# The conditioning rows of an RWKV gate, moved from the early pairs of heads to the later ones

## The chip, the cores and the metric

The kernel runs on one core of a Trainium2 chip. Its metric is the device time of one execution in microseconds (us), the median over runs. Engines are named as in the profile: PE is TensorE (matmuls; PEld is its weight load), DVE is VectorE, ACT is ScalarE, POOL is GpSimd, SP is SyncE, which here issues nearly all DMAs. Q behind a name (SPq, PEq) is the engine's sequencer, which waits and issues.

## The reference

Two layers of an encoder on 256 tokens of width 2048, float32. Each sublayer is conditioned by a vector `c`: a shift, a scale and a gate, each of width 2048, come from one product with a matrix of 2048 x 6144.

```python
def adaln(x, c, norm_g, ada_w, ada_b):
    m = jax.nn.silu(c) @ ada_w + ada_b
    shift, scale, gate = jnp.split(m[:, None, :], 3, axis=-1)
    return rmsnorm(x, norm_g) * (1.0 + scale) + shift, gate
...
    for layer in range(DEPTH):
        if layer % 2 == 0:
            y = hyena_gla_block(...)      # stage mix
        else:
            y = rwkv7_block(...)          # stage tm: 32 heads of 64, both directions
        x = x + gate * y
        h, gate = adaln(x, c, ffn_norm_g[layer], ffn_ada_w[layer], ffn_ada_b[layer])
        x = x + gate * sqrelu_mlp(h, ffn_w1[layer], ffn_w2[layer])   # stages f0 and f1
```

In the RWKV stage the gate multiplies the result of the output projection `w_o`, so it is needed only where that sublayer ends.

## The kernel before

**Stages.** The kernel works off `mix`, `f0`, `tm` (RWKV) and `f1`, in this order; names in the profile begin with the stage in which a tile was made (`tm_w`, `f_w`). Weights come in tiles of 128 x 1024 floats (512 KB), are split into a rounded part (ACT, line 465, `wh`) and a rest (DVE, line 466, `wl`), and PE multiplies in three products (lines 510 to 512).

**The conditioning rows.** The product with `silu(c)` isn't done on PE. A third of one sublayer's matrix (shift, scale or gate) is read as 16 blocks of 128 outputs, each in two halves: 32 half-rows of 128 x 1024 floats. `ada_load` (line 327) takes a buffer of the pool `wp` and issues the DMA on SP's queue; `ada_half` (line 362) is one scalar_tensor_tensor on DVE that multiplies the tile with `silu(c)` and sums it up. After eight halves two small DVE instructions (lines 367, 368) finish four columns of the result. Up to `AP` = 5 half-rows are loaded ahead of the one that is summed.

**The pool `wp`** has six buffers of 512 KB. The half-rows share it with the streamed weights of the stage: `rw_v` (line 494; values, for the first half of the pairs) and `rw_o` (line 494; output projection, for the second half and the end).

**The pairs.** The part of the stage that the change touches works on 16 pairs of heads, in a pipeline written as nested generators. For each `p`, `weave` lays side by side the rest of the chain of pair `p-1`, the first steps of the chain of pair `p`, the preparation of pair `p+1` (it reads tiles `bk`, `ar`, `N`, `X`, `T`, `a` that SP loaded two pairs ahead), the tail of pair `p-2`, `MT[p]` steps of the streamed projections, and either steps of a matrix inversion (the first three pairs) or conditioning half-rows:

```python
wp = pool("wp", bufs=6)
bg = BG[p] if isinstance(BG, tuple) else BG
...
(self.take(inv, IV), IV) if p * IV < 34 * (4 - IB) else (self.bg_gen(bg), bg) if B0 <= p <= B1 else (None, 1),
```

A chain has four steps; in each PE (line 1561), ACT (1563), PE (1571), DVE (1572, `Q`), PE (1582), DVE (1585 or 1588, `S`), DVE and ACT (1590, 1591, back into `Q`) take turns. DVE also masks the products of the preparation (line 1506, `M`) and does parts of the tail (980 to 981, 1632 to 1652).

**Order.** The generators record the work; a list scheduler then orders each engine's instructions by its own timeline, with the chains at higher priority. The order within an engine is fixed when the program is built. At run time an engine waits at its next instruction until that one's inputs are there.

When the half-rows are recorded at pair 3, all shifts and scales of `tm` are done. What is left is the gate of `tm` (32 half-rows) and 3 half-rows of the conditioning of `f1`, which are taken from the same list when the gate is finished. After the pairs `spread_gate` (lines 384 to 386: DVE, PE, ACT) spreads the gate over the partitions, and `residual` multiplies with it.

Of the kernel before, what the change touches and what calls it, by code (L numbers as in the profile page):

```python
# [29 lines left out]
HA, HB, HN, HT = 1000, 1000, 0, 0  # L30
LG, MK, XS, TB, DU, RP, IB, L1, MP, AP = 2, 7, 4, 0, -8.0, 1, 3, 0, 3, 5
W1, W2 = 1, 1
BG, IV, CH, MT, B0, B1, M0, M1, LD = (10, 10, 10, 10, 10, 10, 10, 10, 10, 5, 5, 5, 5, 5, 5, 5, 5, 5), 12, 7, (5, 5, 5, 5, 5, 5, 5, 5, 5, 5, 5, 2, 3, 2, 3, 2, 3, 2), 3, 14, 6, 6, 6
PK, PF = 8, 3
RH, ZZ = (0, 2.4, 2, 2), 0
NF, F1, TF = 2, 2, 0
# [1689 lines left out]
```

## Time and profile before

| what | value |
|---|---|
| median of 3 runs | 3052.12 us (3045.83 to 3054.84) |
| the profiled execution's own time | 3047.34 us |
| its span, first to last instruction | 3045.3 us |
| mean granted TensorE clock | 0.973 |
| busy share of PE, DVE, ACT, POOL | 94%, 70%, 43%, 17% |
| bytes moved, mean rate | 752.30 MB, 247 GB/s |
| the pairs | from about 1807 us to 2231 us of the span |
| the 35 half-rows of the change on DVE | from 1902.7 us to 2048.4 us |

The page gives busy time by engine; windows of the span give busy time, granted clock (1.00 is full), share of the DMA engines' time and GB/s by stretch; the lists of waits name who waited, for whom, the total in us, the number of times and the longest; an instruction's idle time stands in brackets behind it in the timeline, with what ended it.

### The profile page before, as it was taken

How to read it: one execution, taken by the hardware profiler on the slowest of the kernel's cores; microseconds unless marked ns; L12 is line 12 of the kernel's file. 1: busy time of each engine (PE TensorE's matmuls, PEld its weight loads, DVE VectorE, ACT ScalarE, POOL GpSimd, SP SyncE). 2: the span in 40 equal slices, each digit the busy share in tenths (PEclk: the TensorE clock that was granted, in tenths of full speed). 3: DMA queues.
4: the chain of work that ended last, by engine and by line, in shares of the span. 5: the costliest groups of instructions: out<-in, count | busy, mean ns of one | idle time of the engine just before them, and what ended most of it. 6: DMA issues, size and time to landing. Idle time of an engine off the chain costs nothing. (4 is left out here: it accounts for less than half of the span.)

```text
span 3045.3 us, 52042 instructions
## 1 busy us (share of the span) xinstructions
PE 2871.4 (94%) x20308; PEld 2488.7 (82%) x20308; DVE 2122.1 (70%) x3126; ACT 1301.6 (43%) x1947; POOL 522.2 (17%) x574
## 2 busy tenths in 40 slices
PE   6999989999999999997999878999998999999998
PEld 2678776789988999886888777777778998899986
DVE  7899866657777788787768875775646776455454
ACT  3233334444443444443466542334445443344443
POOL 1211200011100011004354541322322110001000
PEclk9999999999999999998999987999999999999999
DMA  9978777747898988984987788997545777555552
GB/s 328 326 271 284 243 262 263 247 154 244 287 308 306 304 290 290 313 297 158 323 264 249 266 258 226 301 300 208 149 149 194 245 252 272 193 186 183 202 193 93
DMA packets 279970, 752.30 MB, mean 247 GB/s; under 512 B 73081, under 2 KB 99577, under 8 KB 278572
## 3 DMA queue, kind: packets, MB, share of 16 engines
q1 hardware_dynamic: 279148, 745.38, 73.1%
q8 instruction: 159, 2.61, 0.3%
q10 hardware_dynamic: 576, 3.60, 0.3%
q14 instruction: 87, 0.71, 0.1%
HBM read 706.08 MB, written 42.80 MB: 246 GB/s over the span
## 5 line engine op out<-in xcount | busy, mean ns | idle before, releaser
L466 DVE TENSOR_TENSOR f_wl<-f_w,f_wh 128x1024 fp32r<-128x1024 f32 x512 | 630.8, 1233 | 444.3 <-ACT f_wh L465 433.4
L465 ACT CAST f_wh<-f_w 128x1024 fp32r<-128x1024 f32 x512 | 538.0, 1052 | 748.4 <-PE f_mm L512 315.8
L511 PE MATMUL f_mm<-f_h,f_wh 128*128 128x256 f32 x2048 | 579.5, 283 | 0.0
L510 PE MATMUL f_mm<-f_h,f_wh 128*128 128x256 f32 x2048 | 579.5, 283 | 0.0
L512 PE MATMUL f_mm<-f_h,f_wl 128*128 128x256 f32 x2048 | 579.1, 283 | 0.0
L511 PE MATMUL f_mm<-f_wl,f_hid 128*128 128x512 f32 x1024 | 398.6, 389 | 1.1 <-DVE f_wl L466 1.1
L512 PE MATMUL f_mm<-f_wh,f_hid 128*128 128x512 f32 x1024 | 398.5, 389 | 0.0
L511 PEld LDWEIGHTS f_mm<-f_h,f_wh 128*128 128x128 f32 x2048 | 393.2, 192 | 0.1
L510 PEld LDWEIGHTS f_mm<-f_h,f_wh 128*128 128x128 f32 x2048 | 393.0, 192 | 0.1
L512 PEld LDWEIGHTS f_mm<-f_h,f_wl 128*128 128x128 f32 x2048 | 392.9, 192 | 0.0
L510 PE MATMUL f_mm<-f_wh,f_hid 128*128 128x512 f32 x1024 | 357.9, 389 | 0.0
L362 DVE SCALAR_TENSOR_TENSOR mix_w<-mix_w,mix_s 128x1024 f32<-128x1024 f32 x175 | 219.8, 1265 | 77.0 <-DMA mix_w<-in_ada_f 52.5
L466 POOL TENSOR_TENSOR f_hid<-f_u,f_hid 128x512 fp32r<-128x512 f32 x64 | 98.0, 1531 | 990.6 <-ACT f_hid L465 988.2
L362 DVE SCALAR_TENSOR_TENSOR f_w<-f_w,mix_s 128x1024 f32<-128x1024 f32 x174 | 233.6, 1345 | 2.6 <-DMA f_w<-in_ada_f 2.6
L511 PEld LDWEIGHTS f_mm<-f_wl,f_hid 128*128 128x128 f32 x1024 | 192.2, 188 | 41.3 <-DVE f_wl L466 1.7
L512 PEld LDWEIGHTS f_mm<-f_wh,f_hid 128*128 128x128 f32 x1024 | 192.3, 188 | 39.8
L510 PEld LDWEIGHTS f_mm<-f_wh,f_hid 128*128 128x128 f32 x1024 | 192.2, 188 | 39.7
L466 DVE TENSOR_TENSOR tm_wl<-tm_w,tm_wh 128x1024 fp32r<-128x1024 f32 x128 | 164.4, 1287 | 85.8 <-ACT tm_wh L465 81.6
L465 ACT CAST mix_wh<-mix_w 128x1024 fp32r<-128x1024 f32 x114 | 119.4, 1050 | 201.2 <-PE mix_mm L512 86.3
L510 PE MATMUL tm_mm<-tm_x,tm_wh 128*128 128x256 f32 x512 | 161.2, 316 | 12.3 <-DMA tm_x<-mix 10.8
L465 ACT CAST tm_wh<-tm_w 128x1024 fp32r<-128x1024 f32 x128 | 133.4, 1046 | 86.7 <-PE tm_mm L511 60.3
L466 DVE TENSOR_TENSOR mix_wl<-mix_w,mix_wh 128x1024 fp32r<-128x1024 f32 x114 | 142.4, 1254 | 38.8 <-ACT mix_wh L465 38.7
(456 smaller groups left out, 5494.6 us busy)
## 6 DMA issues: line engine op xcount, KB each, us to landing
f_w<-in_w SPq DMA_DIRECT2D x512, 512.0 KB, 5.1
f_w<-in_ada_f SPq DMA_DIRECT2D x125, 512.0 KB, 5.6
mix_w<-in_ada_mix SPq DMA_DIRECT2D x96, 512.0 KB, 6.2
mix_w<-in_w_in SPq DMA_DIRECT2D x80, 512.0 KB, 5.0
mix_w<-in_ada_f SPq DMA_DIRECT2D x64, 512.0 KB, 5.2
tm_x<-mix SPq DMA_DIRECT2D x64, 512.0 KB, 5.8
f_w<-in_ada_tm SPq DMA_DIRECT2D x49, 512.0 KB, 5.8
mix_w<-in_w_out SPq DMA_DIRECT2D x32, 512.0 KB, 4.6
```

Source lines behind the costliest of these rows:

```text
L362: V.scalar_tensor_tensor(w, w, 1.0, self.s[:, j * (D // 2) : (j + 1) * (D // 2)], ALU.mult, ALU.mult, accum_out=a[:, j, i : i + 1])
L465: c = self.nc.scalar.copy(hi, a)
L466: d = (eng or self.nc.vector).tensor_tensor(lo, a, hi, ALU.subtract)
L510: mm(out, lhsT=l[0], rhs=r[0], start=start, stop=False)
L511: mm(out, lhsT=l[0], rhs=r[1], start=False, stop=False)
L512: mm(out, lhsT=l[1], rhs=r[0], start=False, stop=stop)
```

## The change

One line of constants: how many half-rows go with each pair, and from which pair to which.

```diff
-BG, IV, CH, MT, B0, B1, M0, M1, LD = (10, 10, 10, 10, 10, 10, 10, 10, 10, 5, 5, 5, 5, 5, 5, 5, 5, 5), 12, 7, (...), 3, 14, 6, 6, 6
+BG, IV, CH, MT, B0, B1, M0, M1, LD = 5, 12, 7, (...), 8, 15, 6, 6, 6
```

`MT` is the same on both sides. Before, pairs 3 to 5 get ten half-rows each and pair 6 the last five; in the change pairs 8 to 14 get five each. The number of instructions on each engine is the same: 35 half-rows are moved, with their 35 DMAs and the small instructions behind them. What the scheduler makes of it is shown in three places.

**DVE, around pair 6 (counted from 0, as all pairs here).** `tm_w_18704` and `tm_w_18748` are tiles of half-rows; `tm_wl` are rests of `rw_v` weights; `tm_gn` and `tm_o` are of a tail. Before:

```order
L466 TENSOR_TENSOR tm_wl_18777<-tm_w_18672,tm_wh_18776 128x1024
L362 SCALAR_TENSOR_TENSOR tm_w_18704,tm_as_18151<-tm_w_18704,mix_s_96 128x1024
L1506 TENSOR_TENSOR tm_M_18792<-tm_mm_18794,tm_rc_11838 128x4x2x64
L1640 TENSOR_SCALAR tm_gn_18887<-tm_mm_18851 128x256
L362 SCALAR_TENSOR_TENSOR tm_w_18748,tm_as_18151<-tm_w_18748,mix_s_96 128x1024
L466 TENSOR_TENSOR tm_wl_18911<-tm_w_18674,tm_wh_18910 128x1024
```

In the change:

```order
L1506 TENSOR_TENSOR tm_M_18723<-tm_mm_18725,tm_rc_11838 128x4x2x64
L1588 SCALAR_TENSOR_TENSOR tm_S_18751<-tm_ps_18746,tm_pc_17599,tm_SP_18580 128x64 x2
L1591 COPY tm_Q_18001<-tm_S_18751 64x128
L1585 TENSOR_TENSOR tm_S_18783<-tm_ps_18778,tm_pc_17976 128x128
L1591 COPY tm_Q_18349<-tm_S_18783 64x128
L1640 TENSOR_SCALAR tm_gn_18809<-tm_mm_18776 128x256
L466 TENSOR_TENSOR tm_wl_18830<-tm_w_18613,tm_wh_18829 128x1024
```

The two half-rows ahead of the mask `M` and of the third `wl` are gone from there; the first of the 35 now comes some seven rows further down.

**DVE, around pair 10.** Before, no half-row stands there:

```order
L1506 TENSOR_TENSOR tm_M_20210<-tm_ps_20211,tm_rc_11838 128x4x2x64
L466 TENSOR_TENSOR tm_wl_20254<-tm_w_20119,tm_wh_20253 128x1024
L1506 TENSOR_TENSOR tm_M_20210<-tm_ps_20212,tm_rc_11838 128x4x2x64
L1572 TENSOR_SCALAR tm_Q_19841<-tm_ps_20226 64x128
L1588 SCALAR_TENSOR_TENSOR tm_S_20238<-tm_ps_20233,tm_pc_19106,tm_SP_20084 128x64 x2
L1591 COPY tm_Q_19499<-tm_S_20238 64x128
L1640 TENSOR_SCALAR tm_gn_20296<-tm_ps_20263 128x256
L1585 TENSOR_TENSOR tm_S_20270<-tm_ps_20265,tm_pc_19474 128x128
```

In the change:

```order
L466 TENSOR_TENSOR tm_wl_20152<-tm_w_20009,tm_wh_20151 128x1024
L1572 TENSOR_SCALAR tm_Q_19719<-tm_ps_20124 64x128
L1506 TENSOR_TENSOR tm_M_20108<-tm_ps_20110,tm_rc_11838 128x4x2x64
L362 SCALAR_TENSOR_TENSOR tm_w_20566,tm_as_20023<-tm_w_20566,mix_s_96 128x1024
L1588 SCALAR_TENSOR_TENSOR tm_S_20136<-tm_ps_20131,tm_pc_19008,tm_SP_19974 128x64 x2
L1591 COPY tm_Q_19377<-tm_S_20136 64x128
L1640 TENSOR_SCALAR tm_gn_20197<-tm_ps_20164 128x256
L362 SCALAR_TENSOR_TENSOR tm_w_20613,tm_as_20023<-tm_w_20613,mix_s_96 128x1024
L1585 TENSOR_TENSOR tm_S_20171<-tm_ps_20166,tm_pc_19352 128x128
L1506 TENSOR_TENSOR tm_M_20178<-tm_ps_20179,tm_rc_11838 128x4x2x64
```

Half-rows now stand between the steps `S`, `Q` and `M` of two chains; the next two follow within eight rows more.

**SP, the queue of DMAs, at the same place.** Before, SP issues the `rw_o` weights four in a row, ahead of the loads for a later pair:

```order
L494 DMA tm_w_20251<-in_rw_o 128x1024
L494 DMA tm_w_20362<-in_rw_o 128x1024
L494 DMA tm_w_20522<-in_rw_o 128x1024
L494 DMA tm_w_20636<-in_rw_o 128x1024
L1458 DMA tm_pc_20155<-ab_11797 64x2x4 x2
```

In the change:

```order
L494 DMA tm_w_20554<-in_rw_o 128x1024
L327 DMA tm_w_20566<-in_ada_tm 128x1024
L327 DMA tm_w_20613<-in_ada_tm 128x1024
L327 DMA tm_w_20695<-in_ada_tm 128x1024
L1458 DMA tm_pc_20383<-ab_11798 64x2x4 x2
L327 DMA tm_w_20771<-in_ada_tm 128x1024
L1453 DMA tm_ar_20379<-ab_11798 128x2x512
L1452 DMA tm_bk_20380<-ab_11798 128x2x512
```

Loads of half-rows now stand ahead of the loads of the pair's tiles. By the addresses in the built program, at this place `rw_o` tiles that wait for their use (`tm_w_20149`, `20266`, `20432`, `20554`) hold four of the six buffers. `tm_w_20566` takes the buffer of the half-row `tm_w_20494`, `tm_w_20613` that of the weights `tm_w_20009` (split in the rows above), `tm_w_20695` that of `20566`, `tm_w_20771` that of `20613`: two buffers go round. The order on PE differs only in a few places among the first eight pairs; from pair 10 on it is the same.

More of the change, by code (lines that the diff above doesn't have):

```diff
@@ L32 @@
 W1, W2 = 1, 1
-BG, IV, CH, MT, B0, B1, M0, M1, LD = (10, 10, 10, 10, 10, 10, 10, 10, 10, 5, 5, 5, 5, 5, 5, 5, 5, 5), 12, 7, (5, 5, 5, 5, 5, 5, 5, 5, 5, 5, 5, 2, 3, 2, 3, 2, 3, 2), 3, 14, 6, 6, 6
+BG, IV, CH, MT, B0, B1, M0, M1, LD = 5, 12, 7, (5, 5, 5, 5, 5, 5, 5, 5, 5, 5, 5, 2, 3, 2, 3, 2, 3, 2), 8, 15, 6, 6, 6
 PK, PF = 8, 3
```

## The prediction

> **What bounds the kernel now.** First the page: PE is busy nearly the whole span.
>
> ```profile
> span 3045.3 us, 52042 instructions
> PE 2871.4 (94%) x20308; PEld 2488.7 (82%) x20308; DVE 2122.1 (70%) x3126; ACT 1301.6 (43%) x1947; POOL 522.2 (17%) x574
> ```
>
> So a moved piece of DVE and DMA work is worth what PE's idle time changes. Next the windows, first over the stretch that holds the half-rows, the one that gets most of them, and the rest of the pairs; then by 10 us around the one real hole. Columns: window, its length, busy us of PE, PEld, DVE, ACT and POOL, granted clock, DMA share, GB/s.
>
> ```profile
> 1900.00:2050.00 150.00, 143.40 (x1799) 119.69 (x1799) 115.79 (x239) 57.31 (x146) 42.93 (x63) 0.97 0.95 296
> 2050.00:2160.00 110.00, 108.81 (x1401) 83.59 (x1395) 66.17 (x153) 51.48 (x134) 34.71 (x60) 1.00 0.75 217
> ...
> 1980.00:1990.00 10.00, 6.52 (x50) 5.75 (x50) 5.34 (x8) 2.58 (x3) 0.59 (x1) 0.94 0.83 244
> 1990.00:2000.00 10.00, 10.00 (x120) 8.33 (x118) 5.51 (x11) 2.50 (x8) 1.62 (x6) 0.55 0.95 325
> ```
>
> From 1900 to 2050 us PE is idle 6.6 us (150 less 143.4), and the DMA engines are full (0.95). From 2050 to 2160 us PE is idle 1.2 us, DVE has 44 us free and DMA a quarter. Third, whom PE waited for between 1950 and 2000 us, and what the half-rows cost DVE and ACT from 1900 to 2050 us (who, for whom, us, times, longest):
>
> ```profile
> PE tm_mm L1561 <- DVE tm_M L1506: 3.5, 1, 3.5
> PE tm_mm L510 <- ACT tm_wh L465: 1.3, 1, 1.3
> ...
> DVE tm_w L362 <- DMA tm_w<-in_ada_tm: 13.1, 8, 4.7
> ...
> ACT tm_wh L465 <- DMA tm_w<-in_rw_v: 5.5, 3, 2.2
> ```
>
> The longest of these, in DVE's timeline (start, duration, instruction, idle time before it):
>
> ```profile
> 1981.94 1.23 DVE L466 TENSOR_TENSOR tm_wl<-tm_w,tm_wh 128x1024 fp32r<-128x1024 f32 x1
> 1987.83 1.23 DVE L362 SCALAR_TENSOR_TENSOR tm_w<-tm_w,mix_s 128x1024 f32<-128x1024 f32 x1 [4.66 <-DMA tm_w<-in_ada_tm]
> 1988.98 0.08 DVE L362 DVE_READ_ACCUMULATOR tm_w<-tm_w,mix_s 128x1 f32 x1
> 1988.98 0.69 DVE L1506 TENSOR_TENSOR tm_M<-tm_mm,tm_rc 128x512 f32<-128x512 f32 x1
> ```
>
> A half-row whose DMA was late held DVE for 4.66 us; the mask `M` queued behind it, and PE waited 3.5 us for `M`. In the 10 us after that the clock was 0.55.
>
> **Removed: the hole.** In the change no half-row stands on DVE or on the DMA queues there. PE's 6.6 us of idle time were ended by `M` behind a half-row, by `wh` behind a late `rw_v` load, and by chain steps on ACT behind DVE; with 18.4 MB less (35 x 512 KB) in a stretch that moves 44 MB, the `rw_v` loads are not late either. The slow clock costs 10 us x 0.45 = 4.5 us. Gain: 6.6 + 4.5 = 11.1 us at most; I take all of it, since nothing else is named in the holes. Lower end: 6 us, if the `rw_v` waits stay.
>
> By the Trainium skill, page "TensorE: Matmul & The Clock Gate", section Part 1, the array falls to half clock after an idle window of about 3.4 us and comes back after as long a busy one; the 3.48 us hole and the 0.55 behind it agree. By that rule a shorter hole costs only itself.
>
> **Moved: the 35 half-rows.** The DVE work itself is unchanged:
>
> ```profile
> L362 DVE SCALAR_TENSOR_TENSOR tm_w<-tm_w,mix_s x35: 1203/1218/2136, 1902.7 to 2048.4; 128x1024 f32<-128x1024 f32 x35
> L327 SPq DMA_DIRECT2D tm_w<-in_ada_tm x31: 327/382/1363, 1902.4 to 2027.9; - x31
> DMA to landing us min/median/max: 3.5/6.6/10.3
> ```
>
> 35 x 1.22 = 43 us on DVE, 29 of the 35 rows between 2050 and 2160 us (found by laying the new order over the old times): 35 us into 44 free ones. Counted as work alone that costs PE nothing. SP's 35 issues of 0.38 us are 13 us in either place. What counts is whether each tile has landed when DVE comes to it. The landing time there, from the `rw_o` loads of 2060 to 2160 us and then of 2160 to 2250 us, which have the same size:
>
> ```profile
> DMA to landing us min/median/max: 3.1/5.1/8.2
> ...
> DMA to landing us min/median/max: 3.7/4.2/5.1
> ```
>
> Before, at least three buffers went round for the half-rows. In the change two do, since early `rw_o` loads hold the others. So a half-row can only be issued when the last reader of its buffer has ended, and DVE may come to it 0.4 us (issue) plus the landing time later. With the rows' bytes added (217 GB/s plus 29 x 0.524 MB in 110 us = 138, less 10 for two `rw_o` loads that fall outside: 345 GB/s, above the 296 at which DMA was 0.95 busy) I take the median of the full stretch, 6.6 us: 7.0 us in all. What the new order allows, read from the old times of the neighbours at pair 10:
>
> ```profile
> 2079.49 0.69 DVE L1491 COPY tm_Q<-tm_ps 64x512 f32<-64x512 f32 x1 [4.92 <-PE tm_ps L1489]
> ...
> 2083.28 1.22 DVE L466 TENSOR_TENSOR tm_wl<-tm_w,tm_wh 128x1024 fp32r<-128x1024 f32 x1
> 2084.41 0.68 DVE L1506 TENSOR_TENSOR tm_M<-tm_ps,tm_rc 128x512 f32<-128x512 f32 x1
> 2085.01 0.27 DVE L1572 TENSOR_SCALAR tm_Q<-tm_ps 64x128 f32<-64x128 f32 x1
> ...
> 2087.30 0.42 DVE L1640 TENSOR_SCALAR tm_gn<-tm_ps 128x256 f32<-128x256 f32 x1 [1.35 <-PE tm_ps L1637]
> ...
> 2089.38 0.42 DVE L980 SCALAR_TENSOR_TENSOR tm_gn<-tm_gn 128x256 f32<-128x256 f32 x1
> ...
> 2091.99 0.28 DVE L1572 TENSOR_SCALAR tm_Q<-tm_ps 64x128 f32<-64x128 f32 x1
> ```
>
> Half-row 20494 stands behind the first of these rows (ends at 2081.4), 20566 behind the second `M` and `Q` (2085.3), 20613 behind line 1640 (2087.7), 20695 behind line 980 (2089.8), 20771 behind the last `Q` (2092.3). 20566 may start at 2081.4 + 7.0 = 2088.4, so DVE waits 3.1 us. 20613 has the buffer of the weights whose split ends at 2084.5: ready at 2091.5, place 2087.7 + 3.1 = 2090.8, wait 0.7. 20695: ready 7.0 behind 20566's end of 2089.6, at 2096.6, place 2089.8 + 3.8 = 2093.6, wait 3.0. 20771: ready 7.0 behind 20613's end of 2092.7, at 2099.7, place 2092.3 + 6.8 = 2099.1, wait 0.6. Together 7.4 us in four rows, 1.85 each; with a landing of 5.1 us the same steps give 1.6, 2.3, 1.5 and 0.6, together 6.0, or 1.5 each; with 4.2 us 0.7, 0.7, 0.7 and nothing, about 0.5 each. Over the 35 rows, 17 stand as close behind the last reader of their buffer as these (under about 5 us); the first is 19755 at 1998 us, the last 21945 at 2155 us. So DVE waits 17 x 1.85 = 31 us, with bounds of 17 x 0.5 = 9 and of 35 x 1.85 = 65.
>
> How much of a wait on DVE reaches PE? Before, the 13.1 us went with 6.6 us of idle PE: 0.5. Later DVE is further ahead, for it is itself waiting for PE there (2050 to 2160 us):
>
> ```profile
> DVE tm_Q L1491 <- PE tm_ps L1489: 15.2, 5, 4.9
> DVE tm_Q L1572 <- PE tm_ps L1571: 9.4, 10, 1.7
> ```
>
> That lets some short waits vanish, but two buffers leave no reserve behind one; I keep 0.5: 31 x 0.5 = 15.5 us. Bounds: 9 x 0.25 = 2, and 65 x 0.5 = 32.
>
> **Also moved, at no cost.** The DVE part of the spread of the gate now comes right behind the last half-row of the gate; PE reads it only here, some 80 us later, and that is the cover:
>
> ```profile
> L385 PE MATMUL tm_ps<-tm_u,mix_ones x32: 272/275/377, 2232.0 to 2253.8; 128*128 128x128 f32 x32
> ```
>
> The `rw_o` loads lose two or three buffers, but stand 30 to 70 us ahead of their split; nothing. On SP a half-row's DMA that waits for its buffer holds the loads of the pair's tiles behind it (`ar`, `bk`, `X`). Those are issued two pairs ahead, so a few us are covered; a longer block belongs to the slow rival.
>
> **The sum.** 15.5 - 11.1 = +4.4 us on an execution of 3047.34 us (span 3045.3). That one lies 4.8 us under the median of 3052.12, so the median comes to 3056 us. That is within 0.3%, 9 us, which is about what a measurement of this kernel can tell from no change.
>
> **The rivals.** *Slower: one late load delays the next.* With two buffers each late half-row delays the next load as well, and while SP waits for the buffer, the loads of `a`, `X`, `bk` for the next pairs wait too; waits then come in lumps of over 3 us, each with a slow clock behind it. For it: 345 GB/s is more than DMA moved over 1900 to 2050 us, landings reach 10.3 us, and the lump of before made 13.1 us of waits cost 11.1 us, 0.85. Against it: before, SP never waited long for a half-row's buffer:
>
> ```profile
> SPq L327 <- DVE tm_w L362: 3.7, 5, 1.1
> ```
>
> Price: 31 x 0.85 = 26 us, less 11.1: +15, 3067 us; with 43 us of waits, as landings of 8 us would make them, +26, 3078 us. It decides when landings come to 8 us or PE shows a second hole of over 3 us.
>
> *Faster: the loads land in time.* Where DMA isn't full, the 512 KB land in 4.2 us, and the scheduler has put the rows where it expects them. For it: a quarter of DMA is free, 40% of DVE too. Against: two buffers, and 345 GB/s. Price: DVE waits 9 us, 2 us reach PE, -9, or -11 if none does: 3042 us.
> By the Trainium skill, page "DMA: Bandwidth & Descriptors", section "Anatomy of one DMA", a transfer takes about 2.0 us plus bytes over 436 GB/s, an estimate of 3.2 us here; by that nearly every half-row would be in time and this rival would hold. The trace's smallest landing, 3.1 us, agrees; its medians of 4.2 to 6.6 do not.
>
> *That the half-rows don't move* is excluded by the order.
>
> **The numbers.** The forecast, within 0.3% (3043 to 3061 us): 0.48. Slower rival, from 3061 to 3078 us: 0.34, since the two buffers and the full DMA follow from the order and only the share that reaches PE is open. Faster rival, under 3043 us: 0.18. The range to hold 8 times in 10 reaches from 3041, where all 11 us are kept, to 3076, and takes in both rivals' prices but for the slower one's end.
>
> **What would show it.** Between 1900 and 2000 us PE busy without the hole, no clock of 0.55 and DMA at some 0.6: the gain. Between 2000 and 2160 us a wait of line 362 for the half-rows of 20 to 35 us in 12 or more times, landings near 6 us, DMA near 1.0, and PE idle 10 to 16 us, in pieces of 1 to 2 us behind `Q`, `S` and `M`: the cost. From 2160 us on the same work as before. The forecast is wrong if line 362 hardly waits (faster), or if it waits as said and PE shows holes of over 3 us with a slow clock (slower).

## The result, and the profile after

| what | before | after |
|---|---|---|
| median, six runs each | 3050.81 us (3041.51 to 3055.93) | 3070.39 us (3061.55 to 3076.67) |
| ratio after to before | | 1.0065, 95% interval 1.0048 to 1.0083 |
| span of the profiled execution | 3045.3 us | 3069.5 us |
| waits of DVE line 362 for half-rows, to 2300 us | 13.1 us in 8 | 31.3 us in 18 |

The change makes the kernel 0.65% slower, 20 us in the medians: inside the range, near the slower rival's 3067 us, and not at the 3056 us that the prediction took.

First where the 24.2 us between the two spans arose. The copy of line 1491 on DVE stands once in each pair's preparation, 16 times in all. Here are the last 13 of them, from the fourth pair on, first for before and then for after (columns: count, shortest, median and longest in ns, start of the first and of the last in us):

```profile
L1491 DVE COPY tm_Q<-tm_ps x13: 694/694/695, 1898.6 to 2187.0; 64x512 f32<-64x512 f32 x13
```

```profile
L1491 DVE COPY tm_Q<-tm_ps x13: 694/695/695, 1900.7 to 2211.6; 64x512 f32<-64x512 f32 x13
```

These twelve pairs took 288.4 us before and 310.9 after, 22.5 more. Up to the fourth copy the difference is 2.1 us, behind the last one 858.3 against 857.9 us. So the loss lies in the pairs, and the experiments below are compared by their length too: the start of the last copy less that of the fourth.

Second, what the time is made of. One window over all pairs, from the first preparation to the norm of `f1`, before and after (window, length, busy us of PE, PEld, DVE, ACT, POOL, granted clock, DMA share, GB/s):

```profile
1807.30:2300.50 493.20, 459.12 (x5132) 367.54 (x5131) 307.54 (x651) 200.42 (x474) 131.98 (x200) 0.94 0.74 223
```

```profile
1811.50:2325.20 513.70, 469.64 (x5131) 373.69 (x5130) 303.86 (x651) 202.34 (x474) 131.95 (x199) 0.91 0.72 213
```

PE's idle time rose from 34.1 to 44.1 us, and the same 5131 matmuls kept it busy for 469.6 us in place of 459.1, at a clock of 0.91 in place of 0.94. Half of the loss is idle time, half is slower work.

Third, by stretches, and inside the slow one:

```profile
1900.00:2000.00 100.00, 100.00 (x1322) 84.37 (x1322) 53.03 (x118) 43.20 (x109) 25.01 (x45) 1.00 0.80 234
2000.00:2160.00 160.00, 147.13 (x1701) 113.91 (x1699) 108.59 (x232) 59.55 (x149) 44.47 (x65) 0.88 0.81 243
...
2030.50:2040.65 10.15, 10.15 (x87) 8.29 (x87) 8.14 (x16) 4.13 (x10) 3.49 (x5) 0.50 0.81 241
2105.60:2119.20 13.60, 10.40 (x48) 7.50 (x47) 9.27 (x22) 4.01 (x9) 2.92 (x5) 0.50 0.89 279
2143.15:2156.70 13.55, 11.82 (x94) 8.86 (x95) 11.58 (x24) 2.87 (x8) 4.02 (x5) 0.50 0.92 304
2167.05:2180.60 13.55, 11.04 (x68) 8.53 (x68) 12.61 (x35) 3.03 (x9) 2.84 (x4) 0.50 0.88 299
```

The hole before 2000 us is gone: PE is busy for the whole 100 us at full clock. From 2000 to 2160 us it is idle 12.9 us, and DMA is not full (0.81, at 243 GB/s). The last four rows are the stretches at clock 0.50 from 2000 us to 2300 us, 50.85 us together; before had one such stretch from the half-rows, at 1990 us.

Fourth, the waits. The half-rows' sums, what they waited for, and their loads:

```profile
L362 DVE SCALAR_TENSOR_TENSOR tm_w<-tm_w,mix_s x35: 1203/1226/2272, 1984.4 to 2178.2; 128x1024 f32<-128x1024 f32 x35
...
  DMA tm_w<-in_ada_tm: 30.5, 17
  DMA tm_w<-in_ada_f: 0.8, 1
```

```profile
DMA to landing us min/median/max: 3.5/5.1/8.6
```

And SP's queue waiting to issue them, with the engine and instruction whose signal ended the wait:

```profile
SPq L327 <- DVE tm_Q L1572: 7.8, 4, 3.5
SPq L327 <- DVE tm_w L362: 6.4, 5, 3.8
SPq L327 <- DVE tm_S L1588: 5.5, 4, 2.5
SPq L327 <- DVE tm_Q L1591: 4.6, 4, 3.5
```

With two smaller rows (2.1 us behind line 466, 1.4 us behind line 1585) SP stood 27.8 us in 20 places until DVE had come far enough. Only lines 362 and 466 read these buffers on DVE; where a step of a chain is named, it is the DVE instruction whose signal came last by the profile, not the reader itself. One such case, in DVE's timeline and then in PE's (start, duration, instruction, idle time ahead of it):

```profile
2105.84 0.67 DVE L1506 TENSOR_TENSOR tm_M<-tm_ps,tm_rc 128x512 f32<-128x512 f32 x1
2110.72 1.22 DVE L362 SCALAR_TENSOR_TENSOR tm_w<-tm_w,mix_s 128x1024 f32<-128x1024 f32 x1 [4.21 <-DMA tm_w<-in_ada_tm]
2111.87 0.08 DVE L362 DVE_READ_ACCUMULATOR tm_w<-tm_w,mix_s 128x1 f32 x1
2111.87 0.28 DVE L1572 TENSOR_SCALAR tm_Q<-tm_ps 64x128 f32<-64x128 f32 x1
2112.08 0.67 DVE L1506 TENSOR_TENSOR tm_M<-tm_ps,tm_rc 128x512 f32<-128x512 f32 x1
```

```profile
2103.43 0.46 PE L1571 MATMUL tm_ps<-tm_R,tm_X 64*64 64x64 f32 x8 [1.74 <-ACT tm_R L1563]
2112.80 1.22 PE L1637 MATMUL tm_ps<-tm_gn,tm_rc 128*128 128x256 f32 x2 [3.02 <-DVE tm_M L1506]
```

A half-row that landed late held DVE for 4.21 us; the chain's `Q` and the mask `M` stood behind it; PE lost 3.02 us until `M` was done. It is the old hole at a new place, but within a stretch whose clock was slow already.

### The profile page after: what moved, and what is told of

It reads as the page before. It is cut to its first block, busy times and chain, and to the rows that moved or that the text cites. A ratio compares the mean times of both kernels' runs of the same rounds, so it can differ in the third digit from the quotient of the medians.

```text
span 3069.5 us, 52054 instructions
## 1 busy us (share of the span) xinstructions
PE 2881.2 (94%) x20308; PEld 2493.4 (81%) x20308; DVE 2118.5 (69%) x3126; ACT 1304.2 (42%) x1947; POOL 524.4 (17%) x574
```

## The experiments

All were timed in five rounds, in four batches; each ratio is to the kernel before on the same chip. "Pairs" is the length defined above, from one profiled execution each; it is 288.4 us before and 310.9 after. These executions lie up to 7 us off the medians of their runs (e5 7.4 us under, e6 7.1 us over), so a difference of a few us in the pairs counts only where the ratios bear it out.

| run | median us | ratio, 95% interval | pairs us | waits of half-row sums for loads, us |
|---|---|---|---|---|
| e1 more buffers, `rw_o` held back | 3072.99 | 1.0075 (1.0061 to 1.0089) | 308.5 | 19.4 |
| e2 no loads, sums kept | 3048.90 | 0.9992 (0.9982 to 1.0003) | 288.4 | none |
| e3 five per pair from pair 3 | 3052.86 | 1.0010 (0.9998 to 1.0022) | 294.2 | 23.2 |
| e4 ten per pair from pair 8 | 3060.54 | 1.0042 (1.0030 to 1.0054) | 305.1 | 34.9 |
| e5 own buffers | 3046.60 | 1.0000 (0.9988 to 1.0012) | 288.3 | 11.5 |
| e6 x late (control) | 3060.78 | 1.0052 (1.0039 to 1.0065) | 308.7 | 24.9 |
| e7 no half-rows | 3031.30 | 0.9946 (0.9931 to 0.9961) | 273.4 | none |
| e8 loads kept, short sums | 3055.95 | 1.0031 (1.0020 to 1.0042) | 296.2 | 37.2 |
| e11 before, own buffers | 3042.24 | 0.9986 (0.9976 to 0.9996) | 284.5 | 2.1 |
| e12 own buffers, place held | 3055.19 | 1.0019 (1.0010 to 1.0028) | 296.3 | 17.8 |

**More of the six buffers for the half-rows.**

```diff
-            w.append(self.load("rw_o", n, i, [self.wp]))
+            with self.tc.issue_after(self.spill) if self.spill is not None else nullcontext():
+                w.append(self.load("rw_o", n, i, [self.wp]))
-            nc.sync.dma_start(yd[:, p, :], o)
+            self.spill = nc.sync.dma_start(yd[:, p, :], o).ins
```

> The change, with each load of rw_o weights put on SP's queue behind the last y_spill store recorded before it, so that such loads are no longer issued far ahead; by the built order four to five buffers of wp go round for the half-rows in place of two. Place, number and bytes of the half-rows are those of the change. Theory (two buffers: each half-row's load can only start when the one before it in its buffer is summed, DVE waits, PE gets holes and a slow clock): waits of line 362 fall from 31 us to 10 or less, time 3045 to 3056 us. Rival A (DMA rate: too many bytes in this stretch): the bytes are the same, waits of 25 us or more stay, 3064 us or more. Rival B (43 us of sums on DVE between the steps of the chains, late or not): 3064 us or more, with few waits.

It missed: 1.0075. The waits fell to 19.4 us and the pairs by 2.4 us, but the `rw_o` loads were now late themselves. ACT's waits for them between 1990 and 2330 us:

```profile
ACT tm_wh L466 <- DMA tm_w<-in_rw_o: 7.5, 3, 5.2
```

What the pairs gained was lost behind them (the copy of the last pair to the norm of `f1`: 127.5 us, against 113.6). The run doesn't tell the theories apart.

**No loads, the sums kept.** The sums read `silu(c)` twice in place of the tile.

```diff
-                self.nc.sync.dma_start(w, self.A["ada_" + u[0]][u[1] * KT + i][:, j])
+                if self.wa is None:
+                    self.nc.sync.dma_start(w, self.A["ada_" + u[0]][u[1] * KT + i][:, j])
...
-        V.scalar_tensor_tensor(w, w, 1.0, self.s[:, j * (D // 2) : (j + 1) * (D // 2)], ALU.mult, ALU.mult, accum_out=a[:, j, i : i + 1])
+        sh = self.s[:, j * (D // 2) : (j + 1) * (D // 2)]
+        V.scalar_tensor_tensor(w, w if self.wa is None else sh, 1.0, sh, ALU.mult, ALU.mult, accum_out=a[:, j, i : i + 1])
```

> The change, but the 35 half-rows of the pairs are not loaded: DVE multiplies silu(c) with itself into the same buffers, so the gate is wrong. 18.4 MB and the waits for them are gone, DVE's work and the buffers' turns stay. Theory (late loads): no wait of line 362, no hole, 3036 to 3046 us, below before. Rival A (DMA rate): the same. Rival B (DVE's sums between the steps of the chains): 3060 us or more.

Without loads and their waits all of the loss is gone: 22.5 us of pairs, 0.0073 of the ratio. But the time came only to that of before, not 11 us below. It lies between what the two theories expected, so the sums are not free at the new place (they stand at 2016 to 2140 us here, closer together than in the change).

**Rate and place apart.**

```diff
-BG, ..., B0, B1, ... = 5, ..., 8, 15, ...
+BG, ..., B0, B1, ... = 5, ..., 3, 14, ...    (e3)
+BG, ..., B0, B1, ... = 10, ..., 8, 15, ...   (e4)
```

> One part of the change alone: five half-rows with each pair, but from pair 3 on as before (pairs 3 to 9). Theory: what hurts is the place, where early rw_o loads hold the buffers; here most half-rows still stand among rw_v loads, DMA is less full than before, and the hole at 1985 us shrinks: 3042 to 3052 us. Rival C (five with each pair, spread over more pairs, is what hurts): 3060 us or more.

> The other part of the change alone: ten half-rows with each pair as before, but from pair 8 on. Theory: the same place, so the same two or three buffers and late loads: waits of line 362 of 25 us or more, 3062 to 3078 us. Rival C (five with each pair is what hurts): 3045 to 3055 us.

Five per pair at the old place cost 5.8 us of pairs (in the ratio not told from before), ten per pair at the new place 16.7 us, both together 22.5 us. The place carries most of it. That the two prices add up to the last digit is chance with one profile each; the ratios give 0.0010 and 0.0042 against 0.0065. Both times lie just outside what the theory expected, e3 0.9 us over its range and e4 1.5 us under.

**Buffers of their own, and a control.** The pool of four needs 16 KB per partition, which the reload of x leaves free until its new place.

```diff
-LG, MK, XS, ... = 2, 7, 4, ...
+LG, MK, XS, ... = 2, 7, 15, ...       (e5 and e6)
...
-                w = self.t(self.wp, [P, D // 2], "w")
+                w = self.t(self.wa or self.wp, [P, D // 2], "w")      (e5)
-                        se.close()
+                        se.close(); sw = ExitStack(); self.wa = self.pool(sw, "wa", bufs=4)
-                        self.open_x(xs, nc.sync)
+                        sw.close(); self.wa = None; self.open_x(xs, nc.sync)
```

> The changed kernel, with a pool of four 512 KB buffers for the half-rows of the pairs alone, so that none of them goes into one of the six that the weights of the V and output projections use; to make room the reload of the 2 MB of x stands with pair 15 and not with pair 4 (the next run does that alone). Same bytes, same sums, at the same pairs. Theory of the buffers (a half-row's load starts only after the row before in its buffer, and two buffers go round): waits of line 362 for its loads fall from 31 us to under 8, idle time of TensorE in the stretch of the pairs falls from 36 to 26-30 us, time 3048-3056. Theory of the DMA rate (17.5 MB more in this stretch beside the other loads is too much at any number of buffers): waits stay at 20 us or more, time 3064-3072. Theory of the sums (35 sums of 1.22 us stand between the steps that TensorE waits for): waits fall, but the time stays at 3060-3070.

> Control for the run with buffers of its own: the changed kernel with the reload of x (2 MB) moved from pair 4 to pair 15, and nothing else. Theory of the buffers and theory of the sums: no change to the changed kernel's 3070, waits of line 362 near 31 us (3066-3074). Theory of the DMA rate: 2 MB leave the stretch before the half-rows and come after it, so no change either. If this run is faster by more than 5 us, the reload's place is part of the next gain, and the run with buffers of its own is read against this one.

With buffers of their own the loss is gone (1.0000 against the control's 1.0052), but not by one cause: with buffers free, the scheduler drew the sums forward, to where they stood before the change (this run's sums):

```profile
L362 DVE SCALAR_TENSOR_TENSOR tm_w<-tm_w,mix_s x35: 1203/1218/1737, 1900.4 to 2065.1; 128x1024 f32<-128x1024 f32 x35
```

So the shared buffers also set the place: in the change the sums stand late partly because no buffer is free earlier. The waits of e5, 11.5 us, were more than the 8 expected at most, and its time lies under the expected 3048 us. The control's ratio can't be told from that of the change, since their intervals overlap.

**Without half-rows, and with short sums.** The first leaves out their loads and sums in the pairs, and so leaves all six buffers to the weights; the second keeps the loads and sums 16 of 1024 columns.

```diff
-                w = self.t(self.wp, [P, D // 2], "w")
+                w = self.t(self.wp, [P, D // 2], "w") if self.wa is None else None    (e7; the DMA as in e2)
...
+        if w is None:
+            V.tensor_scalar(a[:, j, i : i + 1], self.s[:, i : i + 1], 0.5, None, ALU.mult)
...
+        m = 16 if self.wa else D // 2                                       (e8)
-        V.scalar_tensor_tensor(w, w, 1.0, self.s[:, j * (D // 2) : (j + 1) * (D // 2)], ...)
+        V.scalar_tensor_tensor(w[:, :m], w[:, :m], 1.0, self.s[:, j * (D // 2) : j * (D // 2) + m], ...)
```

> The changed kernel with the half-rows of the pairs left out: neither loaded nor summed (a sum of 1 column writes what the next step reads, so the gates are not the reference's). It is the floor that the place of the half-rows can reach, and the run without loads (3048.9) less this one is the price of the sums alone. Theory of the buffers: the sums lie beside other work, price 0-4 us, time 3045-3050. Theory of the sums: they cost 35 x 1.22 = 43 us of VectorE, of which a quarter or more reaches TensorE, time 3030-3040.

> The changed kernel with its half-rows of the pairs loaded and waited for as before, but each summed over 16 of its 1024 columns (the gates are not the reference's). Theory of the buffers: the buffers are free about 1 us earlier per row, but the load still takes 4-6 us behind it, so the waits stay or grow (25-45 us) and the time is 3060-3070. Theory of the sums: VectorE has 40 us less to do in this stretch, time 3045-3055 whatever the waits. Theory of the DMA rate: as the theory of the buffers.

e7 took the time that the theory of the sums expected; e8 lies between the two theories. With e2 these make a square. Over the floor of 273.4 us, the pairs take 15.0 us more with the sums alone (e2), 22.8 us more with the loads and their waits alone (e8), and 37.5 us more with both (the change): 15.0 + 22.8 = 37.8, so the two prices add up about. In the ratios: 0.0046, 0.0085, and together 0.0119 against 0.0131, which the intervals allow. That e7 has the six buffers for the weights alone doesn't show as a price: ACT waits for no `rw_o` tile in e2 either. How the sums reach PE is seen between 2050 and 2150 us, without half-rows and then with the sums alone:

```profile
2050.00:2150.00 100.00, 98.73 (x1287) 75.53 (x1286) 57.77 (x133) 45.02 (x118) 31.45 (x53) 1.00 0.66 188
```

```profile
2050.00:2150.00 100.00, 93.85 (x1138) 70.57 (x1134) 83.94 (x184) 41.47 (x105) 38.18 (x48) 0.97 0.59 162
```

DVE goes from 58% to 84% busy, PE's idle time from 1.3 to 6.2 us, and its clock from 1.00 to 0.97, with no load of a half-row waited for.

Idle time isn't all of the price. From the fourth copy to the last, PE runs the same 3580 matmuls in each of these profiles (windows over the pairs, us):

| run | pairs | PE busy | PE idle | clock |
|---|---|---|---|---|
| e7, no half-rows | 273.4 | 272.1 | 1.3 | 1.00 |
| e2, sums alone | 288.4 | 281.1 | 7.3 | 0.99 |
| the change | 310.9 | 294.2 | 16.8 | 0.92 |
| before | 288.4 | 280.6 | 7.8 | 0.98 |
| e11, before with own buffers (below) | 284.5 | 281.4 | 3.1 | 1.00 |

So the 15.0 us of the sums are 6.0 us of idle time and 9.0 us in which PE is busy for longer; the 22.5 us of the loads are 9.5 us of idle time and 13.0 us of longer busy time, with the clock down from 0.99 to 0.92.

**Own buffers with the sums tied to chain steps.** Two runs tied each sum behind an earlier DVE instruction of a chain.

```diff
-            with self.behind():
+            with self.tc.issue_after(self.vm[-16]) if self.wa else self.behind():      (e9; e10: -4 and BG, B0, B1 = 3, 3, 14)
```

> The run with buffers of its own let the scheduler draw the sums forward to 1900-2066 us, so it undid the place as well as the shortage of buffers. Here the buffers stay (four, x reloaded at pair 15), and each sum is tied behind a chain step's DVE instruction (line 1572) recorded sixteen before, so that the 35 sums stand at chain steps 19 to 47 (the changed kernel: 20 to 48), about one per step and a quarter, and the loads may run ahead. Theory of the buffers: without late loads at the same place the time falls from 3061-3070 to 3042-3052, waits of line 362 under 5 us, no window between 2050 and 2200 us under 47 us of PE in 50. Theory of the place (a sum at pairs 8 to 14 stands worse than at 3 to 9, whatever its load does): waits fall, the time stays at 3055-3065.

> Candidate: as the run before (four buffers of their own, sums tied behind chain steps), with three half-rows per pair from the fourth pair on, tied four steps back: one sum at nearly every chain step from 13 to 55, the last three at the end. Theory of the buffers: no late loads, so at most the price of the sums is left over the floor of 3031-3035: 3038-3048; if the sums' price comes from several in a row between two chain steps (theory of the clusters), one at a time costs less than half of 14 us: 3035-3041. Theory of the place: between, 3045-3052.

They took 3141.58 and 3123.18 us (1.0306 and 1.0256). The tie changed the scheduler's order from before the pairs on; the first copy of line 1491 came at 1874.3 us in e9, against 1810.7 in the change. So both say nothing on place or buffers, and the even spread stays untried.

**Own buffers in the kernel before.** The edit of e5 with `BG`, `B0` and `B1` as before.

> Candidate: the kernel before (ten half-rows from pair 4 on) with the four buffers of their own and x reloaded at pair 15. Theory of the buffers: its 13 us of waits of line 362 and its hole at 1986 us go, 3038-3046. Theory of the sums: the sums stand as before and cost the same, 3044-3052.

This is the fastest of those that compute everything, by a little: 0.9986 (0.9976 to 0.9996). It removes what the prediction called the hole; the sums stand at 1907 to 2066 us, in place of 1903 to 2048:

```profile
1900.00:2050.00 150.00, 149.36 (x1905) 125.41 (x1904) 113.09 (x239) 62.78 (x158) 38.01 (x67) 1.00 0.92 297
```

PE's idle time there fell from 6.6 to 0.6 us, the clock rose to 1.00, and the waits of line 362 fell from 13.1 us to 2.1. Yet the pairs gained 3.9 us, and the ratio says 1 to 7 us. The copies of line 1491 show that most of the gain is lost again soon: right behind the hole e11 is 12.6 us ahead (1996.65 against 2009.29 us), four copies later 3.8 us (2099.95 against 2103.75).

Against the floor, at the same clock of 1.00, PE in e11 is busy 9.3 us longer for the same matmuls. Nearly all of that, 9.0 us (70.7 against 61.7), is on the chain's lines 1561, 1571 and 1582 (1567, 1577 and 1588 in e7), whose single matmuls last as long as there, 227 to 234 ns in the mean: they overlap less. With the sums alone (e2), these lines hold 8.9 of the 15.0 us, 4.5 as busy and 4.4 as idle time. So most of what the sums cost is seen in the chains, in part without any listed idle time; that each such matmul waits for a step on DVE is argued, not shown.

**Own buffers with the place held by data.**

```diff
+                    if p == 6:
+                        for _ in range(4):
+                            nc.vector.tensor_copy(self.t(self.wa, [P, D // 2], "w")[:, :1], Z[5]["S"][2][:, 0, :1])
```

> Tying the sums to chain steps changed the order from before the pairs on, so that run could not separate place and buffers. Here the place is held by data: in the run with four buffers of their own, each buffer first gets one column from the running state of pair 5 (four tiny VectorE copies recorded with pair 6), so no half-row can be loaded before that; nothing else differs. The sums then stand at chain steps 24 to 44 of 64 (the changed kernel: 20 to 48, the kernel before: 8 to 30), and the order is that of the changed kernel up to the middle of the pairs. Same bytes in the same stretch. Theory of the buffers (waits 22 us and sums 14 us over the floor): the waits of line 362 fall from 25-31 us to under 10, the time to 3046-3054, near the run without loads (3049). Theory of the place or of the DMA rate: waits of 15 us or more, or the time stays at 3058-3070.

The time lies just over the end of what the theory of the buffers expected (3055.2 against 3054), and the waits fell less than it said. SP's queue ahead of these loads, and the landing of these loads:

```profile
SPq L327 <- DMA tm_w<-in_ada_tm: 6.2, 5, 1.6
SPq L327 <- DVE tm_w L362: 2.5, 4, 0.9
SPq L327 <- DMA tm_w<-in_rw_o: 1.6, 2, 1.2
SPq L327 <- DVE tm_gn L1646: 0.9, 1, 0.9
```

```profile
DMA to landing us min/median/max: 3.2/7.0/9.8
```

```profile
2008.00:2148.00 140.00, 130.64 (x1532) 101.88 (x1526) 106.75 (x220) 52.72 (x133) 43.34 (x60) 0.92 0.91 280
```

The loads hardly wait for DVE to free a buffer now: 3.4 us in place of 27.8 (and 7.8 us in short waits that the profile puts down to other loads). But they take 7.0 us to land in place of 5.1, by the medians, with the DMA engines 0.91 busy at 280 GB/s, and 17.8 us of waits stay. Against the control the pairs are 12.4 us shorter, the ratio 0.0033 lower (intervals apart); to the run without loads 7.9 us are left. So of the late loads' 20 us or so, about 12 go with the buffers, and the rest stays with four. That the rest is the traffic fits the landing time but wasn't tested alone, and this run's sums stand somewhat earlier and closer (chain steps 24 to 44, against 20 to 48).

## Why the prediction was right or wrong

The range held, but the 3056 us did not: the range took in the price of the slower rival, and it was needed.

**The waits of DVE: the total right, in part by luck.** 17 rows and 31 us were forecast; 17 rows of the gate waited 30.5 us, and one more row 0.8. But the landing was 5.1 us, not 6.6, and DMA moved 243 GB/s there, not 345. For 5.1 us the prediction's own steps give 1.6, 0.7, 1.5 and 0.6 us, 4.4 in four rows (its 2.3 holds the first wait a second time, and for 4.2 us the last is 0.6, not nothing), so 19 us in 17 rows. They also leave out that each 1.22 us sum pushes the rows behind it back, which makes the waits shorter still. What made up the rest isn't shown row by row. The trace shows that the loads were issued late: SP stood 27.8 us behind DVE for them, and the loads of other tiles in the same queue waited too (line 1452 for 8.4 us between 2000 and 2180 us). That the loads stand behind the last reader of a buffer is seen on SP's queue, and e12 shows it to be a cause, as far as its somewhat different place allows.

**How much of a wait reaches PE: the slow clock was left out.** 0.5 of 31 us was taken, 15.5 us. The loads and their waits cost 22.5 us of pairs (the change less e2) or 22.8 (e8 less e7), 0.72 and 0.61 of the 31.3 and 37.2 us waited. As idle time alone the share was lower than forecast, 9.5 us of 31.3 or 0.3. In the other 13.0 us the same matmuls kept PE busy for longer, at a clock of 0.92 in place of 0.99, and the sum put a slow clock at the new place at nothing, since it took a short hole to cost only itself.

**The hole: seen as said, worth less.** PE is busy throughout 1900 to 2000 us, as forecast (the DMA share came to 0.80, not 0.6). But 11.1 us was not its price. At the old place, own buffers (with x reloaded later) removed the hole and most waits for 3.9 us (e11): idle time fell by 4.7 us, but the same matmuls kept PE busy 281.4 us at clock 1.00, no less than the 280.6 us before at 0.98. What the change gained by leaving the old place is more than that, 15.0 us (before less the floor), since the sums there cost 11.1 us too (e11 less the floor), which they then cost again.

**The sums: not free, but nearly as dear before.** "Counted as work alone that costs PE nothing" rested on 44 us of free DVE time against 35 us of sums. With no load waited for, 35 sums cost 15.0 us of pairs. Free time of an engine on average is not free time between two steps of a chain that PE waits for: 24.6 of those 44 us were waits for PE by the prediction's own rows, and 1.22 us put there can delay the step that PE's answer releases. As the sums cost 11.1 us at the old place, only 3.9 us of this is part of the loss, and the ratios (0.9986 and 0.9992) don't tell even that from nothing.

**The sum, set right.** In lengths of the pairs: leaving the old place -15.0 (3.9 for the waits, 11.1 for the sums), the new place +37.5 (15.0 for the sums, 22.5 for the loads): +22.5 us, against +4.4. Of the 18.1 us between, 7.2 lie at the price of the hole, 7.0 at the price of the waits and 3.9 at the sums. What decides is what late loads cost: 4 us at the old place and 22 at the new one, where the prediction had 11.1 and 15.5.

**The rivals.** The slower rival's time was right, 3067 us, and its mechanism in part: waits of line 362 with SP held behind buffers, and slow clock among them. Of its lumps of over 3 us four came on DVE (3.24, 3.28, 3.10 and 4.21 us), and two of these had no slow clock behind them; PE had one such hole, of 3.02 us. The pair's tile loads that SP held up made PE wait 0.2 us in all and DVE not at all. Its terms were off on both sides, 26 us where the loads cost 22.5, and 11.1 where the hole was worth 3.9. The faster rival is refuted: the loads weren't in time. By the Trainium skill, page "DMA: Bandwidth & Descriptors", section "Anatomy of one DMA", 3.2 us was the estimate for such a load; the page fits its rule to DMAs issued from GpSimd, and these are issued on SP. Medians of 5.1 us here and 7.0 us with four buffers say that in a full stretch the measured rows must be used.

## What to carry to other kernels

Moving background loads to a stretch with a quarter of DMA free didn't help here, where they shared buffers with earlier loads that hold them: count the buffers that go round, and see what the queue of DMAs waits for. Background work on an engine in the critical chain has a price even with its data there, here 0.4 us of the chain for each 1.22 us sum, and "40% idle" doesn't cover it. To price a hole, take away its cause alone and time that: idle time and slow clock that disappeared at one place (11 us by the profile) were worth 4 us at the end.

## What the runs showed of the hardware

The clock fell without a long hole. In the change the stretch at 0.50 from 2105.6 us began behind a hole of 1.74 us that ended at 2103.43, and was there already when the 3.02 us hole opened at 2109.8; at 2030.5 us PE was busy for all of the 10.15 us at clock 0.50, and the idle times shown in PE's timeline ahead of it were 0.99 and 0.42 us:

```profile
2028.61 0.46 PE L1582 MATMUL tm_ps<-tm_Q,tm_bkt 128*64 128x64 f32 x8 [0.99 <-ACT tm_Q L1573]
2030.36 0.66 PE L1561 MATMUL tm_mm<-tm_Q,tm_M 128*64 128x64 f32 x8 [0.42 <-ACT tm_Q L1590]
```

By the Trainium skill, page "TensorE: Matmul & The Clock Gate", section Part 1, half clock follows an idle window of about 3.4 us, and the prediction drew from it that a shorter hole costs only itself. The trace of the change doesn't agree: all four stretches at 0.50, of 10 to 14 us, began behind or in shorter holes, the other two behind 1.61 and 1.11 us and in one of 1.73 us. Holes of this size can thus be dearer than their own length. What the gate counts, no run here settles.

More loads at once did not land sooner: with four buffers in place of two the median from issue to landing went from 5.1 us to 7.0.
